# A decode step's TensorE operands at other SBUF offsets: low weight halves at 64, rows of x at 60, 128 and 112 modulo 256 bytes

## The chip, the core and the metric

The kernel runs on one core of one Trainium2 chip. The metric is device time in microseconds (us), the median of the runs shown. TensorE is called PE here, VectorE DVE, ScalarE ACT, GpSimd POOL and SyncE SP, as in the profile.

## The reference, cut to what matters

The reference is one layer of a hybrid decoder: a prompt of 16 meta and 256 prompt tokens, and 8 sequences of 4 tokens, 304 rows in all, of width 2048. The large products are these, all in float32:

```python
z  = rms_norm(x, norm_mix) @ w_in            # 2048 -> 7456 columns
h  = x + concat([o_a, o_b]) @ w_out          # two mixers: RWKV-7 and retention
hn = rms_norm(h, norm_ffn)
h  = h + (silu(hn @ w_gate) * (hn @ w_up)) @ w_down    # 2048 -> 5632 -> 2048
y  = rms_norm(h, norm_final)
```

## The kernel before, in words

The activations lie transposed, with the 2048 features as 16 tiles of 128 partitions (`KT`) and the 304 tokens (`T`) along the free dimension. A weight tile of 128 x 128 is the stationary operand of a matmul, the token rows are the moving one, and the sum over the 16 tiles gathers in a PSUM bank (`acc`).

PE multiplies in float32r. To keep float32's accuracy, every operand is split into a high half (rounded to float32r by a copy on ACT) and a low half (what is left, a subtraction on DVE). So each step of the large products is three matmuls, in `main` (line 713):

```python
self.pe.matmul(acc[:m, :n], hi[:, o:o + m], xh, start=k == 0, stop=False)
self.pe.matmul(acc[:m, :n], hi[:, o:o + m], xl, start=False, stop=False)
self.pe.matmul(acc[:m, :n], lo[:, o:o + m], xh, start=False, stop=k == K - 1)
```

The weights stream from HBM as 128 x 512 blocks (`wr`, five buffers, line 683). `cast` (line 692) makes the high half `wh` on ACT and `rest` (line 707) the low half `wl` on DVE, five buffers of 2048 bytes per partition each. Four weight tiles of 512 bytes lie in one block, so every tile of a buffer starts at the same offset modulo 256 bytes. While a matmul streams its rows, the weights of the next one are loaded (the profile's PEld).

The program has four kinds of large products, in this order:

- The **mixed stages**, until about 600 us: the input projection, with the mixers' small matmuls (into the banks `mm`) between. The rows of x are in `xh` and `xl`, 16 tiles of `XW` = 320 columns (1280 bytes, five times 256), which start at column `FIRST`. Most projections take all 304 columns; two of the three low-rank tiles take 290 (from column 14) and those of the queries and gates 288 (from column 16, `META`).
- The **output projection**, two halves of 16 tiles, 288 columns. Its rows (the mixers' outputs) are put over x in the same tiles by `fill` (line 1782), at column `SHIFT_X`. For the next product `hn` (line 783) puts the normed h there.
- **gate and up**, 88 tiles of 16 steps, on those same rows, 288 columns.
- **down**, in 11 steps of four feature tiles. Its rows are made by `gu_post` (line 1851) as tiles `act` in the float32r arena, at column `SHIFT_A`.

What sets the order of all this is a planner (`Plan`, line 324) that drafts the program once with estimated costs and then writes the instructions in the drafted order; it does not look at addresses. Tiles of the four pools (`lows`, `const`, `weights`, `scratch`) lie in SBUF one behind the other in the order in which they are first asked for, each start rounded up to 32 bytes. So the size of a small tile ahead decides the offset of all that follow. The tiles `gap` are never read or written: they only take up room. The arena's tiles lie at multiples of 32 bytes.

Every instruction of the program is recorded under line 319, the helper through which all of them are issued, so the profile is read by tiles.

Of the kernel before, what the change touches and what calls it, by code (L numbers as in the profile page):

```python
# [9 lines left out]
F32R = mybir.dt.float32r  # L10
# [5 lines left out]
P = 128  # L16
D = 2048
KT = D // P
# [5 lines left out]
XW = T + 16  # L24
TO = SEQ + NB * NS
# [9 lines left out]
FSTEP = 4  # L35
# [39 lines left out]
NCV = _o  # L75


FIRST = 12
SHIFT_X = [28] * KT
SHIFT_A = [20] * 11  # L80


LASTK = T - P
# [129 lines left out]
def pack(x_prompt, x_sample, state_shift, state_rwkv, state_ret, meta_tokens, norm_mix, w_in,  # L213
# [55 lines left out]
    r = r.reshape(NB // 2, 2, RH, 2, P, RD)  # L269
    out["s0r"] = ca(r.transpose(2, 0, 4, 3, 1, 5))  # L270
    c, rm, cs, _ = constants()
    out["cst"], out["rmask"], out["cs"] = c, rm, ca(cs)
    return out
# [335 lines left out]
class Step:  # L609
# [213 lines left out]
    def start(self):  # L823
        I = self.I
        self.pvt = self.t([P, NPV], "pv", pool=self.cp)
        self.ones = self.t([P, P], "ones", pool=self.cp)
        self.dve.memset(self.ones, 1.0)

        self.omu = self.t([P, 54], "omu", pool=self.cp)
        self.eps = {}  # L830
        for c, e in enumerate((RMS_EPS, GN_EPS, 4 * RMS_EPS), 27):
            self.eps[e] = self.omu[:, c:c + 1]
            self.pool.memset(self.eps[e], e)
        xh, xl = self.xh, self.xl
        warm = self.t([P, 1], "warm")
        self.act.activation(warm, self.ones[:, :1], AF.Tanh)

        gx = self.t([P, KT + KT * T], "xr")
        self.gx = gx[:, :KT]
        xr = self.xr = gx[:, KT:].rearrange("p (k t) -> p k t", t=T)  # L840
        x = lambda a, b: self.sp.dma_start(xr[:, a:b], xT(I)[:, a:b, :])
        self.sp.dma_start(gx[:, :KT + T], I["xT"][:, :KT + T])
        self.load(2)
        x(1, 2)
        self.load(2)
        self.sp.dma_start(self.pvt, I["pv"])
        x(2, 3)
        self.load(2)
        x(3, 4)
        self.load(2)  # L850
        for k in range(4, KT, 2):
            self.load()
            x(k, k + 2)
        self.converted = 0

        pt = self.ps(WARM)
        for _ in range(WARM):
            self.pe.matmul(pt[:, :P], self.ones, self.ones, start=True, stop=True)
# [12 lines left out]
    def constants(self):  # L871

        I, xr = self.I, self.xr
        self.csr = self.t([P, 2, T], "csr")
        self.sp.dma_start(self.csr, I["cs"])
        self.shin = self.t([P, 27, NB], "shin")
        self.sp.dma_start(self.shin, I["shift"])
        o, n = CV["blk"], NCV - CV["blk"]
        self.cst = self.t([P, o], "cst", pool=self.cp)
        self.sp.dma_start(self.cst, I["cst"][:, :o])  # L880
        raw = self.t([P, n], "sums")
        self.sp.dma_start(raw, I["cst"][:, o:])
        sums = self.t([P, P + n], "sums", F32R, pool=self.cp)
        self.act.copy(sums[:, :P], self.ones)
        self.all, self.blk, self.cen = (sums[:, c * P:(c + 1) * P] for c in range(3))
        for g in range(0, KT, 4):
            self.act.activation(xr[:, g:g + 4], xr[:, g:g + 4], AF.Square)
            if g % 8:
                self.dve.tensor_add(xr[:, g - 4:g], xr[:, g - 4:g], xr[:, g:g + 4])
            yield  # L890
        for a, n in (8, 4), (2, 2), (1, 1):
            self.dve.tensor_add(xr[:, :n], xr[:, :n], xr[:, a:a + n])
        self.act.copy(sums[:, P:], raw)
        yield
        yield
        ssq = self.ps(2)
        self.pe.matmul(ssq[:, :T], self.ones, xr[:, 0, :], start=True, stop=True)
        self.rstd1 = self.t([P, T], "rstd")
        yield
        yield from self.rsqrt(ssq[:, :T], 1.0 / D, RMS_EPS, out=self.rstd1)  # L900
        self.dve.tensor_mul(self.csr, self.csr, self.rstd1[:, None, :].to_broadcast([P, 2, T]))
        self.shout = self.t([P, 27, 9], "shout", pool=self.cp)
        self.pool.memset(self.shout, 0.0)

        self.half = self.t([P, 4, 8], "half", pool=self.cp)
        for i, n in enumerate(("w0", "a0", "ka")):
            self.dve.tensor_scalar(self.half[:, i, :], self.pvt[:, PV[n]:PV[n] + 8], 0.5, None, op0=ALU.mult)
        self.dve.tensor_scalar(self.half[:, 3, :], self.pvt[:, PV["ka"]:PV["ka"] + 8], -0.5, 1.0,
                               op0=ALU.mult, op1=ALU.add)
        self.dve.tensor_scalar(self.omu[:, :27], self.pvt[:, :27], -1.0, 1.0, op0=ALU.mult, op1=ALU.add)  # L910
        self.done.add("const")
# [935 lines left out]
    def ffn_jobs(self):  # L1847
        dve, act = self.dve, self.act
        hold = {}

        def gu_post(f, f0, up, acts, last):
            def g(acc):
                t = self.t([P, TO], "fu" if up else "fg")
                dve.tensor_mul(t, acc[:, :TO], self.rstd2)
                yield
                if not up:
                    act.activation(t, t, AF.Silu)
                    hold[f] = t
                    return
                while f not in hold:  # L1860
                    yield
                dve.tensor_mul(t, t, hold.pop(f))
                yield
                s = SHIFT_A[f0 // FSTEP]
                hl = self.t([P, 2, XW], "act", F32R)[:, :, s:s + TO]
                act.copy(hl[:, 0, :], t)
                yield
                dve.tensor_sub(hl[:, 1, :], t, hl[:, 0, :])
                acts[f - f0] = hl[:, 0, :], hl[:, 1, :]
                self.done.add(("act", f))  # L1870
            return g

        def down_post(m, fin):
            def g(acc):
                hm = self.ht[m // 4][:, m % 4, :]
                if fin and m == KT - 1:

                    sq = self.t([P, TO], "sq2")
                    third = [slice(c * TO // 3, (c + 1) * TO // 3) for c in range(3)]
                    for c in third:  # L1880
                        dve.tensor_add(hm[:, c], hm[:, c], acc[:, c])
                    for c in third:
                        act.activation(sq[:, c], hm[:, c], AF.Square)
                    states = self.last_states(0)
                    next(states)
                    yield
                    yield from self.final(sq, states)
                    return
                dve.tensor_add(hm, hm, acc[:, :TO])
                if fin:  # L1890
                    if m == 0:
                        self.ssq3 = self.t([P, TO], "ssq3")

                        root = self.t([P, 1], "root")
                        act.activation(root, self.ones[:, :1], AF.Sqrt)
                    yield
                    yield from self.sumsq(self.ssq3, hm, m == 0)
                    yield
                    act.activation(hm, hm, AF.Copy, scale=self.pv("gfin", m))
            return g  # L1900

        jobs = []
        for f0 in range(0, FT, FSTEP):
            f1 = min(f0 + FSTEP, FT)
            acts = {}
            for f in range(f0, f1):
                for up, name in enumerate(("gate", "up")):
                    jobs.append(Job((name, f), self.xf, gu_post(f, f0, up, acts, f == f1 - 1), cols=(0, TO),
                                    need=lambda: "hs" in self.done, ready="rstd2"))
            for m in range(KT):  # L1910
                jobs.append(Job(("down", f0, m), acts, down_post(m, f1 == FT), cols=(0, TO),
                                need=lambda f=f1 - 1 - (f1 == FT): ("act", f) in self.done))
        return jobs
# [19 lines left out]
    def build(self, gam4):  # L1933
        self.gam4 = gam4
        self.shifts = 0
        self.os, self.on, self.gates, self.ht, self.xs_of = [None] * KT, {}, {}, [], {}
        gap = self.t([P, 56], "gap", F32R, pool=self.lp)
        xh = self.t([P, KT, XW], "xh", F32R, pool=self.cp)
        xl = self.t([P, KT, XW], "xl", F32R, pool=self.cp)
        self.xh, self.xl = xh[:, :, FIRST:FIRST + T], xl[:, :, FIRST:FIRST + T]  # L1940
        self.xf = [(xh[:, k, s:s + TO], xl[:, k, s:s + TO]) for k, s in enumerate(SHIFT_X)]
        self.xs = [(self.xh[:, k, :], self.xl[:, k, :]) for k in range(KT)]
        jobs = [self.z_job(i, self.lora_post(i), c0=META - 2 if i else 0) for i in range(3)]
        for h in range(NPAIR):
# [14 lines left out]
def xT(I):  # L1959

    return I["xT"][:, KT:].rearrange("p (k t) -> p k t", t=T)
# [52 lines left out]
```

## Time and profile before

| what | value |
|---|---|
| median of 3 runs | 1505.85 us (1505.6 to 1507.81) |
| the profiled execution's own time | 1505.9 us |
| its span, first to last instruction | 1504.0 us |
| PE busy | 1489.3 us (99%), 11428 matmuls |
| DVE busy | 1084.7 us (72%) |
| ACT busy | 884.5 us (59%) |
| granted PE clock | 0.999 |

How to read it: the duration of a matmul in the profile runs from its start to the modelled end of its last result, and the matmuls overlap in the pipeline, so durations of some 290 ns add up to more than the time they take. What a matmul costs in a dense run is the distance from its start to the next one's start, called its **pitch** here: the length of a run in the chain of waits, divided by its count.

### The profile page before, as it was taken

The page shows a single profiled execution, that of the slowest core. Times are in us where ns is not written, and L with a number is a line of the kernel's source. Part 1 is how long each engine was busy: PE and PEld are TensorE (multiplying, and loading weights), DVE is VectorE, ACT ScalarE, POOL GpSimd, SP SyncE. Part 2 cuts the span into 40 slices and gives each one's busy share as a digit, 9 for nine tenths or more (in the row PEclk, how much of TensorE's full clock was granted, in tenths as well). Part 3 has the DMA queues.
Part 4 walks back from the last instruction along what each step waited for, and adds up shares of the span by engine and source line. Part 5 has one row for each costly group of instructions (what it writes and reads, how often), then busy time and mean ns, then how long its engine had stood idle before and what let it go on. Part 6 is the DMA issues. An engine that isn't in the chain of part 4 may idle for free.

```text
span 1504.0 us, 31962 instructions
## 1 busy us (share of the span) xinstructions
PE 1489.3 (99%) x11428; PEld 1471.3 (98%) x11428; DVE 1084.7 (72%) x2769; ACT 884.5 (59%) x2109; POOL 32.1 (2%) x165
## 2 busy tenths in 40 slices
PE   9999999999999999999999999999999999999997
PEld 8999999999999989999999999999999999999997
DVE  6989997999999679776656565656565656565656
ACT  6786778787875875567544444444444444444445
POOL 0010000000000000000000000000000000000000
PEclk9999999999999999999999999999999999999999
DMA  7655444545544369857655555555555565555653
GB/s 235 178 143 166 149 155 117 165 156 152 139 124 141 102 221 313 268 173 212 195 175 168 170 170 173 170 170 173 174 167 176 167 174 165 174 169 170 173 170 126
DMA packets 138926, 258.55 MB, mean 172 GB/s; under 512 B 16272, under 2 KB 22928, under 8 KB 138768
## 3 DMA queue, kind: packets, MB, share of 16 engines
q1 hardware_dynamic: 138768, 256.52, 56.3%
q8 instruction: 90, 1.47, 0.4%
q14 instruction: 68, 0.56, 0.1%
HBM read 242.18 MB, written 14.28 MB: 171 GB/s over the span
## 4 chain that ended last, share of the span: by engine, by line
PE 95%; DVE 2%; ACT 1%; issue 0%; DMA 0%; SPq 0%; DVEq 0%; POOL 0%; ACTq 0%
PE acc L319 84%; PE mm L319 11%; DVE arena_dt.float L319 1%; ACT arena_dt.float L319 1%; DVE wl L319 0%; DMA arena_dt.float<-xT 0%; SPq L319 0%; DVE xl L319 0%; ACT arena_dt.float32r L319 0%; ACT wh L319 0%; DVEq L2010 0%; ACT xh L319 0%; POOL arena_dt.float L319 0%; DVE arena_dt.float32r L319 0%; ACT shout L319 0%
## 5 line engine op out<-in xcount | busy, mean ns | idle before, releaser
L319 PE MATMUL acc<-xh,wh 128*128 128x288 f32 (+2 forms) x2592 | 780.7, 301 | 1.8 <-ACT wh L319 1.8
L319 PE MATMUL acc<-xh,wl 128*128 128x288 f32 (+2 forms) x2592 | 762.3, 294 | 0.6 <-DVE wl L319 0.6
L319 PE MATMUL acc<-xl,wh 128*128 128x288 f32 (+2 forms) x2592 | 758.5, 293 | 0.0
L319 ACT CAST wh<-wr 128x512 fp32r<-128x512 f32 (+1 forms) x827 | 504.5, 617 | 343.7 <-PE acc L319 305.8
L319 DVE TENSOR_TENSOR wl<-wr,wh 128x512 fp32r<-128x512 f32 (+1 forms) x827 | 559.3, 685 | 121.3 <-ACT wh L319 116.7
L319 PEld LDWEIGHTS acc<-xh,wh 128*128 128x128 f32 x2592 | 486.3, 188 | 6.1 <-issue 2.7
L319 PEld LDWEIGHTS acc<-xl,wh 128*128 128x128 f32 x2592 | 487.0, 188 | 3.0 <-issue 1.9
L319 PEld LDWEIGHTS acc<-xh,wl 128*128 128x128 f32 x2592 | 485.6, 187 | 1.8 <-DVE wl L319 1.4
L319 PE MATMUL acc<-arena_dt.float32r,wh 128*128 128x288 f32 x1408 | 273.7, 292 | 0.2 <-DVE arena_dt.float L319 0.2
L319 PEld LDWEIGHTS acc<-arena_dt.float32r,wh 128*128 128x128 f32 x1408 | 223.5, 188 | 0.6 <-DVE arena_dt.float L319 0.4
L319 PE MATMUL acc<-arena_dt.float32r,wl 128*128 128x288 f32 x704 | 205.8, 292 | 0.0
L319 DVE TENSOR_TENSOR arena_dt.float<-acc,arena_dt.float 128x288 f32<-128x288 f32 (+4 forms) x181 | 72.6, 419 | 147.9 <-PE acc L319 147.4
L319 DVE TENSOR_TENSOR arena_dt.float<-arena_dt.float 128x288 f32<-128x288 f32 (+21 forms) x658 | 159.3, 278 | 8.6 <-ACT arena_dt.float L319 6.3
L319 PE MATMUL mm<-arena_dt.float 128*128 128x128 f32 (+7 forms) x1120 | 162.2, 299 | 2.2 <-ACT arena_dt.float L319 1.2
L319 ACT ACTIVATE arena_dt.float<-arena_dt.float 128x288 f32<-128x288 f32 (+7 forms) x229 | 97.2, 432 | 103.1 <-DVE arena_dt.float L319 101.6
L319 DVE TENSOR_TENSOR arena_dt.float<-arena_dt.float,acc 128x288 f32<-128x288 f32 (+1 forms) x210 | 94.4, 451 | 87.7 <-PE acc L319 85.2
L319 PEld LDWEIGHTS mm<-arena_dt.float 128*128 128x128 f32 (+1 forms) x1120 | 138.3, 181 | 8.8 <-ACT arena_dt.float L319 1.9
L319 PEld LDWEIGHTS acc<-arena_dt.float32r,wl 128*128 128x128 f32 x704 | 132.3, 188 | 0.0
L319 ACT COPY arena_dt.float<-mm 64x64 f32<-64x64 f32 (+11 forms) x338 | 94.9, 289 | 42.3 <-PE mm L319 38.4
L319 ACT COPY arena_dt.float<-arena_dt.float 128x8 f32<-128x8 f32 (+8 forms) x267 | 62.5, 283 | 27.6 <-DVE arena_dt.float L319 26.3
L319 ACT CAST arena_dt.float32r<-arena_dt.float 128x288 fp32r<-128x288 f32 (+6 forms) x117 | 49.7, 429 | 40.3 <-DVE arena_dt.float L319 39.9
L319 DVE TENSOR_TENSOR arena_dt.float32r<-arena_dt.float,arena_dt.float32r 128x288 fp32r<-128x288 f32 (+6 forms) x116 | 52.1, 451 | 18.3 <-ACT arena_dt.float32r L319 18.0
(68 smaller groups left out, 570.1 us busy)
## 6 DMA issues: line engine op xcount, KB each, us to landing
wr<-big SPq DMA_DIRECT2D x823, 256.0 KB, 2.8
arena_dt.float<-s0r SPq DMA_DIRECT2D x24, 512.0 KB, 6.1
out_rts<-arena_dt.float SPq DMA_DIRECT2D x16, 512.0 KB, 4.4
arena_dt.float<-s0w SPq DMA_DIRECT2D x16, 256.0 KB, 3.3
arena_dt.float<-xT SPq DMA_DIRECT2D x4, 576.0 KB, 6.3
arena_dt.float<-lora SPq DMA_DIRECT2D x16, 128.0 KB, 2.6
out_rws<-arena_dt.float SPq DMA_DIRECT2D x8, 256.0 KB, 3.4
arena_dt.float<-xT SPq DMA_DIRECT2D x6, 304.0 KB, 5.5
```

The source lines that it names most:

```text
L319: return self._plan.keep(f(*a, **k))
```

## The change

It alters where operands start, in bytes per partition. The starts below follow from the order and sizes of the tiles; all are modulo 256.

| operand | before | after |
|---|---|---|
| `wh`, high halves of weights | 64 | 64 |
| `wl`, low halves of weights | 96 | 64 |
| `xh` and `xl`, mixed stages, 304 columns | 144 | 60 |
| the same, 290 columns | 200 | 116 |
| the same, 288 columns | 208 | 124 |
| `xh`, output projection, gate and up | 208 | 128 |
| `xl`, output projection, gate and up | 208 | 112 |
| `act` high, down | 208 | 128 |
| `act` low, down | 208 | 112 |

The float32r arena starts at 128 modulo 256 in both, and the `wr`, `wh` and arena tiles keep their places to the byte: the 56 columns of filler are only split (16 ahead of `wl`, 40 behind `shout`), and two small tiles (`half` and `omu`) move. `act` becomes one flat tile of 640 columns of which the two halves are cut at 0 and 316. On every engine the program has the same instructions in the same order, with the same waits, as before.

```diff
-FIRST = 12
-SHIFT_X = [28] * KT
-SHIFT_A = [20] * 11
+FIRST = 7
+SHIFT_X = 24, 20
+SHIFT_A = 0, 316
...
-        self.omu = self.t([P, 54], "omu", pool=self.cp)
...
-        self.half = self.t([P, 4, 8], "half", pool=self.cp)
+        gap = self.t([P, 40], "gap2", pool=self.cp)
...
-                s = SHIFT_A[f0 // FSTEP]
-                hl = self.t([P, 2, XW], "act", F32R)[:, :, s:s + TO]
-                act.copy(hl[:, 0, :], t)
+                hl = self.t([P, 2 * XW], "act", F32R)
+                hi, lo = (hl[:, s:s + TO] for s in SHIFT_A)
+                act.copy(hi, t)
                 yield
-                dve.tensor_sub(hl[:, 1, :], t, hl[:, 0, :])
-                acts[f - f0] = hl[:, 0, :], hl[:, 1, :]
+                dve.tensor_sub(lo, t, hi)
+                acts[f - f0] = hi, lo
...
-        gap = self.t([P, 56], "gap", F32R, pool=self.lp)
+        self.half = self.t([P, 4, 8], "half", pool=self.lp)
+        gap = self.t([P, 16], "gap", pool=self.lp)
+        self.omu = self.t([P, 54], "omu", pool=self.cp)
...
-        self.xf = [(xh[:, k, s:s + TO], xl[:, k, s:s + TO]) for k, s in enumerate(SHIFT_X)]
+        self.xf = [tuple(v[:, k, s:s + TO] for v, s in zip((xh, xl), SHIFT_X)) for k in range(KT)]
```

## The prediction

> **What bounds the kernel now.** I read the page's engine lines first, then the costliest groups with their forms kept apart, then the chain of waits, and last the timeline at two places. The page says that PE is the bound:
>
> ```profile
> span 1504.0 us, 31962 instructions
> PE 1489.3 (99%) x11428; PEld 1471.3 (98%) x11428; DVE 1084.7 (72%) x2769; ACT 884.5 (59%) x2109; POOL 32.1 (2%) x165
> PE 95%; DVE 2%; ACT 1%; issue 0%; DMA 0%; SPq 0%; DVEq 0%; POOL 0%; ACTq 0%
> ```
>
> PE is busy for 99% of the span and is 95% of the chain that ended last. Nothing else can move the time much, so the change is worth what it does to the distance between matmuls. The groups say how many matmuls there are of each width (count, busy us, mean ns of one):
>
> ```profile
> L319 PE MATMUL acc<-xh,wh 128*128 128x288 f32 x1920 | 569.5, 297 | 0.3 <-ACT wh L319 0.3
> L319 PE MATMUL acc<-xh,wl 128*128 128x288 f32 x1920 | 561.1, 292 | 0.4 <-DVE wl L319 0.4
> L319 PE MATMUL acc<-xl,wh 128*128 128x288 f32 x1920 | 557.4, 290 | 0.0
> L319 PE MATMUL acc<-arena_dt.float32r,wh 128*128 128x288 f32 x1408 | 273.7, 292 | 0.2 <-DVE arena_dt.float L319 0.2
> L319 PE MATMUL acc<-arena_dt.float32r,wl 128*128 128x288 f32 x704 | 205.8, 292 | 0.0
> L319 PE MATMUL acc<-xh,wh 128*128 128x304 f32 x512 | 162.0, 316 | 0.0
> L319 PE MATMUL acc<-xl,wh 128*128 128x304 f32 x512 | 153.8, 300 | 0.0
> L319 PE MATMUL acc<-xh,wl 128*128 128x304 f32 x512 | 153.6, 300 | 0.0
> L319 PE MATMUL acc<-xh,wh 128*128 128x290 f32 x144 | 44.5, 309 | 0.0
> L319 PE MATMUL acc<-xh,wl 128*128 128x290 f32 x144 | 42.9, 298 | 0.0
> L319 PE MATMUL acc<-xl,wh 128*128 128x290 f32 x144 | 42.6, 296 | 0.0
> ```
>
> These durations overlap, so they are no price. The price is the pitch, and it is read from the long runs of the chain (start us, us, what, count):
>
> ```profile
> 63.77 12.82 PE acc L319 x93
> ...
> 604.67 56.48 PE acc L319 x438
> ...
> 719.30 743.59 PE acc L319 x5769
> 1466.43 22.67 PE acc L319 x168
> ```
>
> The run at 63.77 us is 304 columns wide: 12.82/93 = 137.8 ns each. The runs at 604.67 and 719.30 us are 288 wide, output projection in the first, gate, up and down in the second: 56.48/438 = 128.9 and 743.59/5769 = 128.9. The last run is 288 wide too, on rows and weights at the same offsets as before it, and yet, with the last result's 0.29 us taken off, it takes (22.67 - 0.29)/167 = 134.0 ns each.
>
> So the pitch is not a matter of columns alone, and that is what makes an address worth looking at. Two observations bear on it. First, 290 columns from byte 200 last 296 to 309 ns, 288 from byte 208 last 290 to 297: some 6 ns or more for two columns. What a column costs follows from these two groups:
>
> ```profile
> L319 PE MATMUL mm<-arena_dt.float32r 128*128 128x512 f32 x32 | 10.3, 402 | 0.0
> L319 PE MATMUL mm<-arena_dt.float32r 128*128 128x288 f32 x24 | 4.8, 309 | 0.0
> ```
>
> (402 - 309)/224 = 0.42 ns a column, so two columns are worth 0.8 ns; the other 5 come with the start. Second, the same addresses give 128.9 and 134.0: after the interruption just before 1466.43 us the stream settled differently. The pitch is thus set by how the rows' and the weights' streams fall in with each other, and that has more than one steady state.
>
> 288 columns at 0.42 ns are 120 ns, so 9 of the 128.9 are not columns. The Trainium skill ("TensorE: Matmul & The Clock Gate", Back-to-back issue gap) gives N/2.4 + 2.5 ns for matmuls that follow each other, 122.5 ns for 288 columns, and no run here shows so little; by that page 6.4 ns are the most that an address could still give back.
>
> **The change part by part.** All instructions, their order and their waits stay; so nothing is added, removed or queued behind something else, and each term is a count times a difference of pitch.
>
> Rows at 128 and 112 behind the mixed stages, weights all at 64. Of the 1920 steps on `xh`, 256 belong to queries and gates (two of each head's six tiles and two gate tiles, 16 tiles by 16 steps) and stay at one offset; 1664 are output projection, gate and up. Down has 704. Three matmuls each: (1664 + 704) x 3 = 7104 at 128.9 ns, 916 us, the largest part of the kernel. Two of three read high rows: 4736.
>
> What they are worth I estimate by counting 64-byte blocks. 1152 bytes from 208 touch 19 of them, 1216 bytes from 144 touch 20, and 128.9/19 = 6.78 and 137.8/20 = 6.89 ns a block: the two long pitches are nearly proportional to blocks, and less well to columns (0.448 and 0.453 ns, where a column is worth 0.42). From 128, 1152 bytes touch 18 blocks, from 112 still 19. So a high-row matmul would be cheaper by 6.8 ns, and in all 4736 x 6.8 = 32.2 us. The other end is not zero but dearer: the 134.0 ns of the last run, +5.1 x 7104 = +36.2 us. No row shows rows at 128 with weights at 64 in a long run. I take half the block gain, -16.1 us: the stream moves in steps (three matmuls take 387 or 402 ns at the same addresses, a step of 15, about what two blocks a triple would save), and a saving of one step may be had in some triples and not in others. That half is a choice between the row that I trust most (128.9, proportional to blocks) and the lack of any row for the pair.
>
> Queries and gates, 768 matmuls of 288 columns, from 208 to 124: 19 blocks before and after, 0; between -6.8 and +5.1 ns, so -5.2 to +3.9 us.
>
> 304 columns, 512 x 3 and 48 more in a bank `mm`, 1584 matmuls, from 144 to 60: 20 blocks before and after, 0. Down to 20 x 6.78 = 135.6 ns, -2.2 x 1584 = -3.5 us; up by the 5 ns that came with the start at 200, +7.9 us. For 200 is 8 past a multiple of 16 and 144 and 208 are multiples of it, and 60 is not. The Trainium skill ("SBUF — State Buffer", Specifications) has lines of 16 bytes and a penalty for each new one; by it a start at 60 costs one more line and speaks against this part.
>
> 290 columns, 480 matmuls, from 200 to 116: neither is a multiple of 16, 0; down to the 128.9 of 288 columns and 0.8, some -5 x 480 = -2.4 us, and up as much.
>
> ACT and DVE write the same tiles at other starts. Should DVE's 823 subtractions for `wl` get longer, PE covers it: DVE is busy 147 of 160 us where it is fullest, and PE has all of them.
>
> ```profile
> 40.00:200.00 160.00, 160.00 (x1216) 157.51 (x1215) 147.31 (x544) 120.00 (x355) 9.66 (x51) 1.00 0.53 162
> L319 DVE TENSOR_TENSOR wl<-wr,wh 128x512 fp32r<-128x512 f32 x823 | 557.7, 686 | 120.5 <-ACT wh L319 115.8 <-PE acc L319 1.3
> ```
>
> In these 160 us (PE, PEld, DVE, ACT, POOL) the 12.7 us that DVE has free, spread over its 544 instructions, are 23 ns each. If all grew by more, DVE would become the bound there; I count nothing.
>
> Sum: 1505.9 us, the profiled execution's own time (span 1504.0 and 1.9 around it, and 0.05 over the median of 1505.85), less 16.1: 1489.8 us.
>
> **The rivals.**
>
> The pitch gets worse. The two streams would settle behind the mixed stages as they did in the last run: 134.0 in place of 128.9 on 7104 matmuls, +36.2 us, 1542.1 us. It decides from a pitch of 129.3 on, since 0.2% of the time is 3 us and that is 0.42 ns on 7104. For it: rows in the arena lie at multiples of 64 already, in short runs. The four matmuls at 447.26 us have their rows at 128, 0, 128 and 128:
>
> ```profile
> 447.13 0.30 PE L319 MATMUL acc<-xh,wl 128*128 128x288 f32 x1
> 447.26 0.70 PE L319 MATMUL mm<-arena_dt.float32r 128*128 128x288 f32 x4
> 447.80 0.29 PE L319 MATMUL acc<-xh,wh 128*128 128x288 f32 x1
> 447.93 0.29 PE L319 MATMUL acc<-xl,wh 128*128 128x288 f32 x1
> ```
>
> They take (447.80 - 447.26)/4 = 135 ns each, not 122, and the `acc` behind them, from 208, is back at 130. Against it: their weights lie at 128, not at 64, four matmuls are too few to settle, and the 20-block rows next to them upset any stream. It has 0.29.
>
> Addresses do nothing. What sets 128.9 or 134.0 would be the history of the stream alone; the 290 columns would be dearer for another reason. 1505.9 us. The Trainium skill ("SBUF — State Buffer", SBUF: two separate sides) says that PE has ports of its own and waits for nobody; by that rule offsets cannot matter, this rival holds, and the 5 ns at start 200 are what in the trace speaks against it. It has 0.13.
>
> Only the mixed stages gain: the triples behind them come to rest on the same step as now, 387 ns, and the 304 and 290 columns reach their lower ends, -3.5 and -2.4. 1500.0 us, 0.12.
>
> **How the numbers follow.** The forecast, that the block count holds in whole or in part behind the mixed stages, has 0.46, with 1467 to 1502 for its own range: from 32.2, 3.5 and 2.4 us of gain to a quarter of the half. With the fourth case, faster is 0.58; same 0.13; slower 0.29, where 0.2% or 3 us either way is about what a measurement of this kernel can tell from no change. The range goes from 1467, all block gains together, to 1524, half of the worse pitch (every other triple), which leaves out about 0.15 above and some 0.05 below.
>
> **What would show it.** The run at 719.30 us in the chain: 126.6 ns each if the forecast holds (128.9 less 16.1 us/7104), 124.4 if whole, 128.9 if nothing, 134.0 if worse. In it the matmuls on high rows should be the shorter ones and `acc<-xl,wh` unchanged. The run at 63.77 us should stay at 137.8. Instruction counts, the chain's shares and DVE's 686 ns should stay. The forecast is wrong if the 288-column pitch behind the mixed stages does not fall, or if it falls as much for the low rows as for the high ones, which would mean that it is not blocks.

## The result, and the profile after

The changed kernel takes 1528.5 us, median of 4 runs (1526.6 to 1529.6), against 1505.7 us for the kernel before on the same chip: a ratio of 1.015 with a 95% interval from 1.014 to 1.016. It is slower, by 23 us. The forecast was 1489.8 us, and 1528.5 lies above the range (1467 to 1524). Of the rivals the first, the worse pitch, came true in kind and in place, at some three fifths of its price.

The profiled execution took 1529.2 us. Its page, for the lines shown of before:

```profile
span 1527.5 us, 31962 instructions
PE 1512.9 (99%) x11428; PEld 1495.2 (98%) x11428; DVE 1086.5 (71%) x2769; ACT 884.2 (58%) x2109; POOL 32.1 (2%) x165
PE 95%; ACT 2%; DVE 1%; issue 0%; DMA 0%; SPq 0%; DVEq 0%; POOL 0%
```

PE is the bound as before, DVE and ACT work as long as before, and the span has grown by 23.5 us. The chain of waits shows where (start us, us, what, count); the row at 391.38 is a stretch of queries and gates:

```profile
65.49 12.70 PE acc L319 x93
...
391.38 5.60 PE acc L319 x42
...
606.97 58.30 PE acc L319 x441
...
723.80 762.80 PE acc L319 x5769
1490.13 22.48 PE acc L319 x168
```

The same stretch of queries and gates in the chain of before:

```profile
389.87 5.43 PE acc L319 x42
```

The long run has 5769 matmuls as before, but at 762.80/5769 = 132.2 ns in place of 128.9. The output projection does the same: 58.30/441 = 132.2. Queries and gates went from 5.43/42 = 129.3 to 133.3 ns. The 304 columns became a little cheaper, 12.70/93 = 136.6 in place of 137.8. By count that makes 7104 x 3.3 = 23.4 us behind the mixed stages, 768 x 4.0 = 3.1 for queries and gates, 1584 x -1.3 = -2.0 for the 304 columns and a few tenths less for the 290.

The rows themselves add up a little differently. The long run takes 19.2 us more. The stretch from the output projection's row to it (604.67 to 719.30 before, 606.97 to 723.80 after) takes 2.2 us more, and the last stretch, which was slow already, 0.2 us less. So from the output projection's row on the change costs 21.2 us. From the first row of 304 columns to there it is 0.6 us. The other 1.7 us of the span's 23.5 lie ahead of that row, and they are not shown to come from the change: the hundredth matmul starts at 19.82 us before and at 21.83 us after, and at 19.96 and 21.49 us in two kernels below whose operands start there as before (those that move one group of down to 144 and to 224).

The groups by form (count, busy us, mean ns of one) show whether the high rows became the shorter ones:

```profile
L319 PE MATMUL acc<-xh,wh 128*128 128x288 f32 x1920 | 573.2, 299 | 0.2 <-ACT wh L319 0.2
L319 PE MATMUL acc<-xh,wl 128*128 128x288 f32 x1920 | 567.5, 296 | 0.3 <-DVE wl L319 0.2
L319 PE MATMUL acc<-xl,wh 128*128 128x288 f32 x1920 | 565.0, 294 | 0.0
L319 PE MATMUL acc<-xh,wh 128*128 128x304 f32 x512 | 160.5, 313 | 0.0
L319 PE MATMUL acc<-xh,wh 128*128 128x290 f32 x144 | 44.5, 309 | 0.0
```

All three 288-column forms on `xh` and `xl` are longer than before (297, 292, 290): by 2 and 4 ns on the high rows and by 4 on the low ones, so the high rows did not become the shorter ones. These durations overlap; the mean distance to the next start in the blocks of gate and up, in the order high weights and high rows, high weights and low rows, low weights and high rows, went from 129.2, 128.3 and 129.2 ns to 131.9, 131.5 and 133.3.

### The profile page after: what moved, and what is told of

It reads as the page before. It is cut to its first block, busy times and chain, and to the rows that moved or that the text cites. A ratio compares the mean times of both kernels' runs of the same rounds, so it can differ in the third digit from the quotient of the medians.

```text
span 1527.5 us, 31962 instructions
## 1 busy us (share of the span) xinstructions
PE 1512.9 (99%) x11428; PEld 1495.2 (98%) x11428; DVE 1086.5 (71%) x2769; ACT 884.2 (58%) x2109; POOL 32.1 (2%) x165
## 4 chain that ended last, share of the span: by engine, by line
PE 95%; ACT 2%; DVE 1%; issue 0%; DMA 0%; SPq 0%; DVEq 0%; POOL 0%
PE acc L319 84%; PE mm L319 11%; ACT arena_dt.float L319 1%; DVE arena_dt.float L319 1%; DMA arena_dt.float<-xT 0%; DVE wl L319 0%; SPq L319 0%; ACT xh L319 0%; ACT wh L319 0%; DVE xl L319 0%; ACT arena_dt.float32r L319 0%; DVEq L2011 0%; POOL arena_dt.float L319 0%; DVE arena_dt.float32r L319 0%; ACT shout L319 0%
## 5 line engine op out<-in xcount | busy, mean ns | idle before, releaser
L319 PE MATMUL acc<-arena_dt.float32r,wh 128*128 128x288 f32 x1408 | 279.9, 294 | 0.1
L319 PEld LDWEIGHTS mm<-arena_dt.float 128*128 128x128 f32 (+1 forms) x1120 | 138.1, 181 | 8.7 <-ACT arena_dt.float L319 1.9
L319 PEld LDWEIGHTS acc<-arena_dt.float32r,wl 128*128 128x128 f32 x704 | 132.2, 188 | 0.0
```

The source lines that it names most:

```text
L319: return self._plan.keep(f(*a, **k))
```

## The experiments

Down has 11 groups of four feature tiles, 192 matmuls each, with blocks of gate and up (384 matmuls) between them. `SHIFT_A` sets the start of down's rows for each group, so one kernel can try ten starts (the eleventh group is the last stretch). Where a table gives a pitch, it is the mean distance of starts over a group or block. The sweeps were run once each, and all pitches are those of the one execution that was profiled. In the windows view they can be read so: a window counts every matmul that overlaps it, so the pitch is the window plus 0.29 us, divided by the count behind PE's busy time (within one count).

**Weights or rows.** Two kernels each undo one half of the change behind the mixed stages. The first moves only the low weights; the filler that is taken from ahead of them is put ahead of `xh`, so that all else keeps its place:

```diff
-        gap = self.t([P, 56], "gap", F32R, pool=self.lp)
+        gap = self.t([P, 48], "gap", F32R, pool=self.lp)
+        gap = self.t([P, 8], "gap3", F32R, pool=self.cp)
```

> Only the low halves of the weights move, from 96 to 64; rows of x and act stay at 144 and 208 as before. Theory W (the loss comes from the low weights lying at the same start as the high ones): the long run of the chain has a pitch of 132.2 ns in place of 128.9, 7104 x 3.3 = 23 us, and queries and gates 133.3 in place of 129.2, 3 us: some 1530 us. Theory R (the loss comes from where the rows start, 128 and 112): 128.9 ns and 1505.7 us. Theory B (only the two together do it): 1505.7 us here and in the next run as well.

Measured: 1515.7 us (1513.9 to 1520.5), ratio 1.007 [1.005, 1.009]. Its chain:

```profile
605.89 56.95 PE acc L319 x438
...
721.43 749.99 PE acc L319 x5769
```

749.99/5769 = 130.0 ns: neither 128.9 nor 132.2. The low weights alone cost 1.1 ns a matmul, 8 us of the some 10.

The second moves only the rows behind the mixed stages, high ones and low ones by a pair of shifts, with `act` as one flat tile as in the change:

```diff
-SHIFT_X = [28] * KT
-SHIFT_A = [20] * 11
+SHIFT_X = (8, 4)
+SHIFT_A = [(0, 316), (0, 316), (0, 316), (0, 316), (0, 316), (0, 316), (0, 316), (0, 316), (0, 316), (0, 316), (0, 316)]
```

> Only the rows behind the mixed stages move, high ones to 128 and low ones to 112; low weights stay at 96, the mixed stages' rows at 144, 200 and 208. Theory R: long run at 132.2 ns, queries and gates unchanged at 129.2, 1505.7 + 23.4 = 1529 us. Theory W: 128.9 ns and 1505.7 us. Theory B: 1505.7 us.

Measured: 1535.6 us (1533.2 to 1536.2), ratio 1.019 [1.018, 1.021]. Its chain:

```profile
606.45 58.80 PE acc L319 x441
...
723.81 769.21 PE acc L319 x5769
1496.55 22.48 PE acc L319 x168
```

769.21/5769 = 133.3 ns: the rows alone cost 4.4 ns, more than the whole change. Theories W, R and B all miss. Added up, the two halves would cost 40 us, and together they cost 23. That alone does not show that the weights' and the rows' starts act together: the last stretch, at the same addresses, takes 132.2 ns once it runs evenly, and in the last experiment below these addresses take 131.1 and 132.2 ns. With 131.1 the two halves would add up, 1.1 and 2.2 ns to 3.3.

**One start after the other.** Two kernels move down's rows, high and low together, with the low weights at 96 and at 64 (the second by the edit of `gap` and `gap3` shown above):

```diff
-SHIFT_A = [20] * 11
+SHIFT_A = [20, 0, 4, 8, 12, 16, 24, 28, 32, 18, 20]
```

> Low weights at 96 as before. Only the rows of down move, high and low ones together, another start in each of the 11 groups of four feature tiles: 208, 128, 144, 160, 176, 192, 224, 240, 0, 200, 208. Gate and up between them stay at 208. Theory R: the groups at 128 and 0, and perhaps all multiples of 64, are at 132 ns or more, others at 128.9. Theory W: all groups at 128.9, but for 200, which may be dearer as the 290 columns are. If the pitch goes with the distance from rows to weights, it should change smoothly or in steps along the groups.

> The same starts of down's rows, with the low weights at 64. Theory W: all groups, and gate and up at 208, at 132 to 133 ns. Theory R: the same pattern along the groups as with the low weights at 96. If distance to the weights counts, the pattern is another one, since two of three matmuls have the weights at 64 in both and one has them 32 nearer.

Measured: 1516.1 and 1519.2 us. Two more took the low weights to 32 and to 160, with the same `SHIFT_A` (the first with `FIRST = 16` too, 304 columns at 160):

```diff
+        gap = self.t([P, 40], "gap", F32R, pool=self.lp)
+        gap = self.t([P, 16], "gap3", F32R, pool=self.cp)
...
+        gap = self.t([P, 8], "gap", F32R, pool=self.lp)
+        gap = self.t([P, 48], "gap3", F32R, pool=self.cp)
```

> Low weights at 32, rows of down together at 208, 128, 144, 160, 176, 192, 224, 240, 0, 200, 208; 304 columns at 160. If the distance of the low weights from the high ones decides by its size (32 in both), the groups read as with the low weights at 96, and gate and up at 208 take 128.9 ns. If low weights at an odd multiple of 32 straddle one more block of 64 and that decides, the same. Theory P: other numbers, gate and up at 129 to 134 ns.

> Low weights at 160, 64 past their old start; rows of down together at 208, 128, 144, 160, 176, 192, 224, 240, 0, 200, 208, mixed stages as before. If starts count modulo 64 in the weights: gate and up at 208 at 128.9 ns, the groups as with low weights at 96. If modulo 128 or 256 or by distance from the high weights: other numbers, 129 to 134 ns.

Measured: 1523.1 and 1528.5 us. The pitch of down by the rows' start and the low weights' start, in ns; behind a comma stands a second or third steady pitch that the same addresses took elsewhere in these runs:

| rows at | `wl` 32 | `wl` 64 | `wl` 96 | `wl` 160 |
|---|---|---|---|---|
| 128 | 132.4 | 131.7, 132.2 | 133.3, 132.6 | 132.9 |
| 144 | 131.8 | 131.1 | 130.4 | 131.1 |
| 160 | 131.2 | 131.7 | 132.2 | 132.2 |
| 176 | 131.1 | 134.6 | 131.1, 133.3 | 131.1 |
| 192 | 132.6 | 133.3 | 131.1 | 131.1 |
| 200 | 134.4 | 136.0 | 135.5 | 134.4 |
| 208 | 131.1 | 130.0, 131.1 | 128.9, 133.3 | 130.4, 131.1, 132.2 |
| 224 | 131.1 | 133.3 | 132.2 | 132.6 |
| 240 | 132.3 | 131.4 | 131.1, 133.3 | 132.2 |
| 0 | 133.3 | 133.3 | 133.3 | 131.1 |

No group but those at 208 took 128.9 ns, so theories R and W fail here too. No column repeats another one, and gate and up at 208 never took 128.9 ns with the low weights at 32 or 160: neither a distance of 32 or 64 in the weights nor the rows' start by itself decides. That leaves theory P, that a pitch belongs to all the starts together. It says the least of them all and is not tested to the end: most cells of the table were entered once, and since a set can have several pitches, a difference of 1 to 4 ns between two columns can also be one of state. At rows 128, 192 and 0, where 1152 bytes touch 18 blocks of 64, the pitch is 131.1 to 133.3 ns and never below the best of 208 in the same column, where they touch 19. The windows of the run with the low weights at 96 (PE, PEld, DVE, ACT, POOL as busy us and count) show rows at 128, gate and up behind them, rows at 224, gate and up behind those, and gate and up behind rows at 240:

```profile
810.00:830.00 20.00, 20.00 (x152) 20.00 (x151) 13.67 (x27) 8.27 (x14) 0.00 (x0) 1.00 0.53 159
835.00:875.00 40.00, 40.00 (x312) 40.00 (x311) 22.19 (x39) 17.92 (x32) 0.00 (x0) 1.00 0.58 171
...
1184.00:1204.00 20.00, 20.00 (x153) 20.00 (x153) 13.83 (x28) 8.42 (x14) 0.00 (x0) 1.00 0.58 159
1210.00:1250.00 40.00, 40.00 (x302) 40.00 (x301) 21.21 (x37) 17.49 (x32) 0.00 (x0) 1.00 0.55 165
...
1286.00:1326.00 40.00, 40.00 (x312) 40.00 (x312) 22.12 (x39) 18.19 (x32) 0.00 (x0) 1.00 0.59 167
```

20.29/152 = 133 ns at 128. Gate and up stand at 208 in all three of their rows, and yet take 40.29/312 = 129.1 ns behind 128 and 240, and 40.29/302 = 133.4 ns behind 224. The granted clock is 1.00 in each.

**High and low rows apart, and starts off a multiple of 16.** Three more kernels vary the low rows alone, the high rows alone (pairs of shifts for high and low, on the flat `act`), and both in steps of 4 bytes:

```diff
+FIRST = 0
+SHIFT_A = [(20, 340), (20, 308), (20, 312), (20, 316), (20, 320), (20, 324), (20, 328), (20, 332), (20, 336), (20, 348), (20, 340)]
```

> Weights at 64 and 96 as before. In down the high rows stay at 208, the low rows start at 208, 80, 96, 112, 128, 144, 160, 176, 192, 240, 208 in the 11 groups; the mixed stages' 304 columns start at 96 (290 at 152, 288 at 160) instead of 144. Theory H (the high rows, read twice a step, decide): all groups at 128.9 ns. Theory P (the pitch belongs to the set of all starts together, in steps of a thirtieth of a cycle or so, and with more than one steady state for a set): groups differ by up to 5 ns, none predictable from the sweep of both. For the 304 columns no theory has a number but the range from 136.0 to 139.4; a multiple of 16 is not expected to leave it.

```diff
+FIRST = 4
+SHIFT_A = [(20, 340), (0, 340), (4, 340), (8, 340), (12, 340), (16, 340), (24, 340), (28, 340), (32, 340), (36, 340), (20, 340)]
```

> As the run before with the halves exchanged: low rows of down at 208, high rows at 208, 128, 144, 160, 176, 192, 224, 240, 0, 16, 208; 304 columns at 112. Theory H: the groups show what the sweep of both together showed with the low weights at 96 (133.3, 130.5, 132.2, 131.1, 131.1, 132.2, 131.1, 133.3 for 128 to 0). Theory P: others, between 126 and 136.

```diff
+FIRST = 8
+SHIFT_A = [20, 17, 19, 21, 22, 23, 27, 31, 1, 3, 20]
```

> Weights as before, rows of down together at 208, 196, 204, 212, 216, 220, 236, 252, 132, 140, 208, none but the first and the last a multiple of 16; 304 columns at 128. Theory S (a start off a multiple of 16 costs one more line): all nine groups some 5 to 7 ns dearer than the groups beside them, 134 to 136 ns, as 200 was. Theory P: some are no dearer than 131.

(No run shows the "thirtieth of a cycle" of the first; many of the pitches lie some 3.3 ns apart in the sum of three matmuls.) Measured: 1512.6, 1515.7 and 1515.9 us. With the high rows at 208, low rows at 80 to 240 give 132.5, 131.1, 131.1, 131.1, 132.0, 131.1, 133.3, 133.3 and 131.9 ns: theory H falls, the low rows count as well, although each is read once a step (high rows at 208 would allow 128.9 or 133.3 ns, and seven of the nine groups took neither). With the low rows at 208, high rows at 128 to 16 give 133.3, 133.3, 132.2, 132.2, 133.4, 133.4, 131.1, 132.2 and 132.2: not the numbers of the sweep of both. The windows of the fine sweep show rows at 196, 204, 212, 216, 220, 236, 252, 132 and 140:

```profile
812.00:832.00 20.00, 20.00 (x150) 20.00 (x148) 13.40 (x26) 8.25 (x14) 0.00 (x0) 1.00 0.54 159
887.00:907.00 20.00, 20.00 (x154) 20.00 (x153) 13.86 (x28) 8.23 (x14) 0.00 (x0) 1.00 0.56 158
962.00:982.00 20.00, 20.00 (x151) 20.00 (x150) 13.47 (x27) 8.00 (x14) 0.00 (x0) 1.00 0.56 158
1038.00:1058.00 20.00, 20.00 (x151) 20.00 (x151) 13.71 (x27) 8.16 (x14) 0.00 (x0) 1.00 0.60 163
1113.00:1133.00 20.00, 20.00 (x155) 20.00 (x154) 14.04 (x27) 8.39 (x14) 0.00 (x0) 1.00 0.59 163
1188.00:1208.00 20.00, 20.00 (x155) 20.00 (x154) 13.91 (x27) 8.08 (x14) 0.00 (x0) 1.00 0.59 168
1262.00:1282.00 20.00, 20.00 (x155) 20.00 (x154) 14.03 (x28) 8.40 (x14) 0.00 (x0) 1.00 0.58 159
1337.00:1357.00 20.00, 20.00 (x150) 20.00 (x149) 13.33 (x27) 8.19 (x14) 0.00 (x0) 1.00 0.56 159
1412.00:1432.00 20.00, 20.00 (x153) 20.00 (x152) 13.66 (x28) 7.99 (x14) 0.00 (x0) 1.00 0.55 158
```

By the mean distance of starts they are 135.6, 132.2, 134.6, 134.2, 131.1, 131.1, 131.1, 135.5 and 133.3 ns. Theory S holds in part: starts that lie 4 or 8 past a multiple of 16 (196, 212, 132; 216 and 200) are the dear ones, 134.2 to 136.0 ns, and starts that lie 12 past (204, 220, 236, 252, 140) are not, 131.1 to 133.3 ns. The 304 columns took 138.6, 138.1, 139.2 and 138.5 ns on average at 96, 112, 128 and 160, with other low weights in the last; 112 is 0.3 ns below the 138.4 of 144, and none is near the 137.0 that 60 takes on the same count.

**What the stream remembers.** That gate and up at 208 took 129.1 or 133.4 ns by what ran ahead of them was tried with the kernel before and one number changed, the start of the third of the 11 groups:

```diff
-SHIFT_A = [20] * 11
+SHIFT_A = [20, 20, 24, 20, 20, 20, 20, 20, 20, 20, 20]
```

> The kernel before with one edit: the rows of the third of down's eleven groups, 192 matmuls, start at 224 instead of 208. Theory M (a set of addresses has more than one steady state, and the stream keeps the one that it enters until other rows come): those 192 at 132.2 ns, and all behind them at 208 stays at 133.3 ns in place of 128.9, to the end of the long run, some 4300 matmuls x 4.4 = 19 us: 1525 us. Theory N (an address sets the pitch, a new state lasts for a short while only): 192 x 3.3 = 0.6 us, with a lag of one block of gate and up 384 x 4.4 = 1.7 us more: 1506.5 to 1508 us.

Measured: 1526.6 us (1525.9 to 1528.1), ratio 1.013 [1.011, 1.015]. The windows show gate and up ahead of the moved group, the group, gate and up behind it, the next group, back at 208, and gate and up 500 us later; the chain gives the whole:

```profile
834.00:874.00 40.00, 40.00 (x313) 40.00 (x312) 22.16 (x39) 18.09 (x32) 0.00 (x0) 1.00 0.59 171
884.00:906.00 22.00, 22.00 (x169) 22.00 (x168) 15.30 (x30) 8.84 (x16) 0.00 (x0) 1.00 0.54 156
910.00:950.00 40.00, 40.00 (x302) 40.00 (x301) 21.08 (x37) 17.55 (x31) 0.00 (x0) 1.00 0.54 166
960.00:984.00 24.00, 24.00 (x182) 24.00 (x181) 16.58 (x32) 9.66 (x17) 0.00 (x0) 1.00 0.57 159
...
1420.00:1460.00 40.00, 40.00 (x302) 40.00 (x301) 24.48 (x46) 16.21 (x27) 0.00 (x0) 1.00 0.57 165
```

```profile
721.48 763.42 PE acc L319 x5769
1488.44 22.67 PE acc L319 x168
```

313 matmuls in 40 us ahead of the group, 302 behind it, and 302 still at the end: theory M. 192 matmuls at another start cost the kernel 20 us, and nearly all of it falls on matmuls whose addresses, order and waits are those of before. The counterpart, 144 in place of 224:

```diff
-SHIFT_A = [20] * 11
+SHIFT_A = [20, 20, 4, 20, 20, 20, 20, 20, 20, 20, 20]
```

> The same with the third group at 144. In the sweep gate and up came back to 128.9 ns behind rows at 144. Theory M: 192 x 1.6 = 0.3 us, everything behind at 128.9 ns: 1506 us. Theory N: the same. If any departure from 208 throws the stream out of its state for good: 1525 us.

Measured: 1506.2 us (1505.9 to 1508.0), ratio 0.9996 [0.9987, 1.0006]; its chain:

```profile
720.41 746.35 PE acc L319 x5788
1467.86 21.94 PE acc L319 x168
```

746.35/5788 = 128.9 ns: not every departure throws the stream out. The last stretch is now 21.94 us in place of 22.67, since behind its interruption this run came to rest at 128.9 and before at 133.3. That is too little to be measured.

**Does 132.2 ns belong to the new addresses?** First the changed kernel with down's rows back at 208:

```diff
-SHIFT_A = 0, 316
+SHIFT_A = 20, 340
```

> The changed kernel with the rows of down alone back at 208 (high and low), low weights still at 64, output projection, gate and up at 128 and 112. If the table of pitches by address carries over: down's 2112 matmuls at 130.0 ns as in the kernel where only the low weights moved, gate and up at 132.2, 1528.5 - 2112 x 2.2 = 1523.8 us; in the second state seen at 208 (131.1 ns) 1526.2 us. If the entry from rows at 128 and 112 leads elsewhere, another value, the same in all ten groups.

Measured: 1523.1 us (1522.9 to 1524.3), ratio to before 1.011 [1.009, 1.012]. Down took 131.1 ns in two of the ten groups and 130.0 in the other eight, gate and up 132.2 in all blocks: the table carries over, with both of its numbers for 208. Then gate and up were entered from ten different starts, with the changed addresses and with the low weights at 96 (the second has `SHIFT_X = (8, 4)` as well):

```diff
+SHIFT_A = [20, 0, 4, 8, 12, 16, 24, 28, 32, 18, 20]
```

> The changed kernel with the rows of down, high and low together, at another start in each group (208, 128, 144, 160, 176, 192, 224, 240, 0, 200, 208), so that gate and up, at 128 and 112 with the low weights at 64, are entered from ten different places. If 132.2 ns belongs to these addresses: gate and up return to it behind every group. If it is one of several states: at least one block of gate and up lies elsewhere, at 130 to 131 ns if a better one exists.

> The same entries with gate and up at 128 and 112 and the low weights at 96. Their last stretch already showed 132.2 ns at addresses that took 133.3 before it, so two states exist: I expect blocks of gate and up at 133.3 and at 132.2 ns, in turns set by the start before. If the entry plays no part, 133.3 everywhere.

Measured: 1530.7 and 1528.1 us. The windows show gate and up at 128 and 112; in the first kernel behind rows at 208, 144, 224 and 240:

```profile
764.00:804.00 40.00, 40.00 (x304) 40.00 (x304) 21.37 (x38) 17.53 (x31) 0.00 (x0) 1.00 0.57 167
916.00:956.00 40.00, 40.00 (x305) 40.00 (x304) 21.38 (x38) 17.53 (x31) 0.00 (x0) 1.00 0.57 167
1222.00:1262.00 40.00, 40.00 (x303) 40.00 (x302) 21.10 (x38) 17.51 (x31) 0.00 (x0) 1.00 0.56 166
1299.00:1339.00 40.00, 40.00 (x304) 40.00 (x303) 21.53 (x38) 17.62 (x32) 0.00 (x0) 1.00 0.56 165
```

and in the second behind rows at 208, 128 and 144:

```profile
764.00:804.00 40.00, 40.00 (x305) 40.00 (x304) 21.59 (x38) 17.56 (x32) 0.00 (x0) 1.00 0.55 165
840.00:880.00 40.00, 40.00 (x307) 40.00 (x307) 21.66 (x38) 17.77 (x32) 0.00 (x0) 1.00 0.55 166
915.00:955.00 40.00, 40.00 (x304) 40.00 (x304) 21.36 (x38) 17.80 (x32) 0.00 (x0) 1.00 0.56 166
```

By the distance of starts the first are 132.2, 132.2, 133.3 and 132.2 ns: nine of the ten blocks came to rest at 132.2, the one behind 224 at 133.3. So the changed kernel sits on the lower of the two pitches that its addresses have shown, and no entry that was tried gave less. The second are 132.2, 131.1 and 132.2: with the low weights at 96 the same rows have three, 131.1, 132.2 and 133.3, and the kernel that moved only the rows sat on the highest. Of the two values expected for the second kernel, 132.2 came (eight of the ten blocks) and 133.3 did not; 131.1 (two blocks) was not expected.

## Why the prediction was wrong

**The bound and the price were right.** PE is 99% busy in both, DVE's and ACT's other starts cost nothing that shows, and nearly the whole difference is pitch times count.

**The step that failed is the count of 64-byte blocks**: "From 128, 1152 bytes touch 18 blocks, from 112 still 19. So a high-row matmul would be cheaper by 6.8 ns". It rested on two pitches, 128.9 and 137.8 ns, that happened to be in the ratio of 19 to 20. Rows at 128, high and low together, take 131.7 to 133.3 ns by the low weights' start, at 0 131.1 to 133.3, and one start has up to three pitches. A count of blocks has no room for either. The prediction's own mark against it came up: all three matmuls of a step became dearer, not the high ones cheaper. The half of the gain that was then taken, -16.1 us, was a middle between a rule and no rule; in its place the starts that were changed to came to rest at 132.2 ns, 3.3 ns dearer, and from the output projection's row on the kernel takes 21.2 us more.

**The rival had the direction and the place, at too high a price.** "The two streams would settle behind the mixed stages as they did in the last run" is right in that they settled at a worse pitch. The hint for it, 135 ns in four arena matmuls at 128 and 0, pointed the right way, which may be luck: four matmuls with weights at other starts show no steady pitch. (The remark against the hint is misread too: the `acc` matmuls beside those four are 288 wide from 208, 19 blocks by the prediction's own count, not 20.) The 134.0 ns was the second pitch of the old addresses (133.3 ns once even, the rest is its first few matmuls). The new addresses have their own, 132.2 and 133.3, and the kernel got the lower: 3.3 in place of 5.1 ns on 7104 matmuls. The remark that the same addresses have more than one steady pitch was the best of the prediction, and was used for a price only, not for the chances: it says that the long run of before sat on the better of the two pitches that its addresses had shown, so a move away from there had more to lose.

**The chances** should have followed from that. The experiments later ran 68 other sets of starts for 288 columns behind the mixed stages (rows high, rows low, low weights), most of them entered once; at their best they took 130.0 to 136.0 ns, 65 of them 131.0 or more, none 128.9. Forecasting any gain behind the mixed stages needed a reason stronger than two numbers in ratio; 0.29 for slower was far too low.

**Addresses do nothing** is refuted by the runs: order and waits stay, and the pitch of 288 columns moves between 128.9 and 136.0 ns. The Trainium skill ("SBUF — State Buffer", SBUF: two separate sides) lets PE wait for nobody. The trace of before agrees as far as other engines go: of 1913 triples of matmuls in the long run 1857 took 386 or 387 ns, while DVE and ACT were now busy, now idle. What the runs add is that PE's own pace hangs on where its operands start.

**The mixed stages** came out inside their bounds. By one stretch of each, queries and gates cost +3.1 us (bounds -5.2 and +3.9); the 304 columns -2.0 us (-3.5 and +7.9); the 290 columns a few tenths less (-2.4 and +2.4). The 5 ns at 200 were rightly put down to the start: down's rows there take 134.4 to 136.0 ns. The fear for 60, that it isn't a multiple of 16, was not borne out. By the rule of the Trainium skill cited in the prediction ("SBUF — State Buffer", Specifications) every start off a line should cost; here the starts 4 and 8 past a line are dear, those 12 past (131.1 to 133.3 ns) lie among the starts on a line, and 60 is 12 past.

**What stays open.** Which part of the machine sets the pitch, and why often in steps of 3.3 ns a triple, isn't shown: the weights' high halves stayed at 64 in all kernels, and no run took the loading of weights away. No rule was found that gives a pitch from the starts; the table is a list. Nor is it known why one entry leads to one pitch and another to the next, only that it does so again: the four runs of the kernel with one group at 224 lie within 2.2 us. No version beats the kernel before: its 128.9 ns is the least of all sets tried, and a last stretch that settles better is worth 0.7 us.

## What to carry to other kernels

When matmuls run back to back, the distance between their starts depends on where rows and weights begin, and one set of starts can have several steady values, chosen by what ran ahead. So the offsets of a kernel that runs at a low pitch are not a place to reason from: price a move by a sweep over whole blocks inside one kernel (ten starts for one run here), enter each start from more than one other, and expect a loss until it shows otherwise. And a small edit is to be judged by the pitch of everything behind it, not by its own matmuls: 192 moved matmuls cost 20 us.

## What the runs showed of the hardware

- The sum of three matmuls of 288 columns often comes to rest on 386.7, 390, 393.3, 396.7 or 400 ns, steps of some 3.3 ns, but not always (gate and up at 208 with the low weights at 160 held 391.2 for four blocks). One stream held its value for over 500 us, through changes between operands at the same starts.
- A steady pitch is the mean of a pattern that repeats. In gate and up the distances of starts run some 127, 138 and 135 ns over and over with only the rows moved, 129 and 131 with only the low weights moved, and in the changed kernel the sums of three run 391, 398, 400 and 398.
- The same starts (rows 208, low weights 96) hold 128.9 or 133.3 ns a matmul; 192 matmuls at 224 switch from the first to the second for good, 192 at 144 don't, and in the sweep 192 at 0 switched as well and 192 at 240 and at 200 led back.
- Of ten starts of 288-column rows off a multiple of 16, those 4 or 8 bytes past one took 134.2 to 136.0 ns, those 12 past 131.1 to 133.3.
- No set came near the 122.5 ns that the formula of the Trainium skill ("TensorE: Matmul & The Clock Gate", Back-to-back issue gap) gives for 288 columns; the least measured is 128.9 ns. That section calls its formula the gap of an isolated matmul, and says that for a stream of weight loads and matmuls it counts too little at small widths and too much at large ones. So the 6.4 ns that the prediction took for the most that an address could give back are no bound by that page.
